# Out-projection weights split once in fp16, other orders and buffers, and the last norm's sums on TensorE

## The chip, the cores and the metric

One Trainium2 chip, one of its cores. The time is the device time of one execution in microseconds (us), the median of several runs. The engines are named as in the profile: PE is TensorE, DVE is VectorE, ACT is ScalarE, POOL is GpSimd and SP is SyncE, which here issues the DMAs, in order, in one queue.

## The reference, cut to what matters

One inference step of one layer with 2048 prompt tokens and 32 sample tokens, 1024 wide:

```python
u = rmsnorm(x, norm_mix_pre)
p = u @ w_in                                   # 3592 columns: two head groups
o_a = rmsnorm(o_a, gdn_norm_w) * silu(z)       # 4 heads of 128, gated delta rule
o_b = rmsnorm(o_b, attn_norm_w)                # 8 heads of 64, banded attention
mix = concat([o_a, o_b]) @ w_out
x = x + rmsnorm(mix, norm_mix_post)
u = rmsnorm(x, norm_ffn_pre)
gate, up = split(u @ w_gate_up)                # 2 x 2816 columns
h = gelu(causal_dwconv(gate) + ffn_conv_b) * up
x = x + rmsnorm(h @ w_down, norm_ffn_post)
```

Results are float32. The kernel multiplies in two fp16 (or fp32r) parts, high and low: a product is the sum of three matmuls, high x high, high x low and low x high.

## The kernel before, in words

Tokens lie along the free dimension, features along the 128 partitions. Mixing runs in four blocks of 512 tokens (the first has the 32 sample tokens too, so 544, done as 2 x 272). After it the FFN runs in blocks of up to 1056 tokens, as a Strassen-like scheme of seven operands a pair of feature tiles; `build_fu` makes them, each as a high part (`fuh`, ACT) and a low part (`ful`, by a subtraction).

The order of all instructions is set when the program is built, by the planner `Sched` (from line 150): streams yield operations, and the one with the earliest estimated start goes next, ties by the number given to `spawn`. `later` and a `slack` hold a PE operation back in the estimate. Every operation passes through line 191, so the profile is read by tile names, not by lines. On the chip each engine runs its own list in order and waits by semaphores; a waiting instruction holds all that are behind it on that engine. `either(wait)` (line 1624) picks DVE or POOL by the planner's estimate.

The streams that matter here:

- `dense_stream` (line 1080): products with w_in per block (kinds G and A), and the out-projection. W(b-1), the out-projection of the block before, stands eight tiles into block b. For the last block it is cut in two: P takes the heads 0, 1, 2, 4, 5 of column tiles 2 to 7 and 0, 1, and Q the late heads 3, 6, 7, in two groups of four column tiles, head by head.
- `class Weights` (line 374): w_out is loaded for each use (70 pieces `wr` of up to 128x512), scaled with the norm weight and split to two fp32r parts: `wh` by ACT, `wl` by DVE. Each out-projection matmul has an operand `oh` or `ol` (the mixed heads, F32R) and one of these.
- `ev_mix` (line 1183) evacuates a column tile of the out-projection, ACT squares it, POOL adds the squares in `acc`, and SP stores the tile in `mixd`. `residual` then sums over partitions on PE (`one,acc`), takes the power on POOL (`rcol`) and adds to x.
- `finish` (line 2339): the final norm of an FFN block. `yacc` holds the result; squares (`fx`, ACT) are added up in `facc`, PE sums over partitions (`one,facc`), POOL takes the power (`fyc`), PE spreads the factor over the partitions (`ident,fyc`), and ACT copies it to `frb` in SBUF. Then each of the 8 tiles is scaled, added to x (`end_x`) and stored. The last block runs in three parts of 512, 256 and 256 tokens. Tiles 2, 4 and 6 go by ACT and POOL, the others by DVE.

The lines of the last block's tiles before:

```python
if fb == last and k in (2, 4, 6):
    yield act(y, y, AF.Copy, scale=f_post[:, k:k + 1])
    yield G.tensor_tensor(y, y, rb[:, c0:c0 + cn], op=OP.mult)
    yield G.tensor_tensor(x[:, :cn], x[:, :cn], y, op=OP.add)
else:
    yield V.scalar_tensor_tensor(y, y, f_post[:, k:k + 1], rb[:, c0:c0 + cn], op0=OP.mult, op1=OP.mult)
    yield V.tensor_tensor(x[:, :cn], x[:, :cn], y, op=OP.add)
```

## Time and profile before

| | |
|---|---|
| median of 3 runs | 2887.34 us (2884.07 to 2887.57) |
| the profiled execution's own time | 2881.63 us |
| its span, first to last instruction | 2879.8 us |
| mean granted TensorE clock | 0.969 |
| busy: PE / DVE / ACT / POOL | 2649.2 / 2096.1 / 1474.0 / 751.7 us |

A share is an average over the span. Mixing lies before about 1451 us, the FFN behind it. In a row of the timeline the first number is the start and the second the duration, and the brackets hold the idle time of the engine ahead of the instruction with what ended it. Where PE is slow because of its clock, the windows say so in the column of the granted clock (1.0 is full speed).

### The profile page before, as it was taken

Reading aid. Unit: us, or ns where it says so; the run is one execution under the profiler, and the core shown is the slowest. Engines: PE = TensorE matmul, PEld = TensorE weight load, DVE = VectorE, ACT = ScalarE, POOL = GpSimd, SP = SyncE. Lnnn points to the kernel's source line nnn. Section 1 sums busy time; section 2 is a strip of 40 time slices with the busy share of each in tenths; the row PEclk is TensorE's granted clock in tenths of the full one; section 3 lists DMA queues with packets and bytes.
Section 4 is the critical chain, followed back from the end, with each engine's and each line's share of the span. In section 5 each row is a group of like instructions: output and inputs, shape, how many; then the busy total and the mean of one; then the engine's idle time right before and its main releaser. Section 6 shows DMA issues by size and latency. Waiting matters only on the chain.

```text
span 2879.8 us, 53610 instructions
## 1 busy us (share of the span) xinstructions
PE 2649.2 (92%) x20044; PEld 1932.2 (67%) x20044; DVE 2096.1 (73%) x4873; ACT 1474.0 (51%) x3077; POOL 751.7 (26%) x982
## 2 busy tenths in 40 slices
PE   6888899999999989999859999999998899999995
PEld 4667658666575656666637787777777768768673
DVE  6878877588867888588688867868687636456467
ACT  5666556455655656466746764736454333223132
POOL 2322232333223421242265332322213000000004
PEclk9999999999999999999979999999999999999997
DMA  5545334575546545574635543434323433223231
GB/s 173 169 97 139 102 100 119 162 160 122 139 120 163 154 104 136 147 182 107 169 116 180 168 144 124 149 107 148 118 94 124 158 98 94 81 71 100 74 122 59
DMA packets 342199, 366.66 MB, mean 127 GB/s; under 512 B 177841, under 2 KB 241585, under 8 KB 341937
## 3 DMA queue, kind: packets, MB, share of 16 engines
q1 hardware_dynamic: 340016, 356.93, 42.9%
q0 software_dynamic: 1920, 6.29, 0.7%
q8 instruction: 157, 2.57, 0.4%
q14 instruction: 106, 0.86, 0.1%
HBM read 227.64 MB, written 98.12 MB: 113 GB/s over the span
## 4 chain that ended last, share of the span: by engine, by line
PE 72%; DVE 13%; ACT 5%; DMA 4%; issue 3%; POOL 2%; SPq 1%; DVEq 0%; ACTq 0%; POOLq 0%
PE pd L191 46%; PE pg L191 16%; PE pss L191 11%; DVE ca L191 1%; ACT wijunk L191 1%; DVE fx L191 1%; DVE wip L191 1%; SPq L191 1%; DVE fy L191 1%; DVE fg L191 1%; DVE xs L191 1%; ACT fcb L191 1%; DMA w6r<-w_gate_up 1%; DMA wir<-w_gate_up 1%; DVE fcb L191 1%
## 5 line engine op out<-in xcount | busy, mean ns | idle before, releaser
L191 PEld LDWEIGHTS <-wip 128*128 128x128 f16 x8004 | 780.0, 100 | 405.3 <-issue 91.4
L191 PEld LDWEIGHTS <-w6p 128*128 128x128 f16 x5436 | 530.1, 98 | 187.3 <-issue 17.9
L191 PE MATMUL pd<-uh,wip 128*128 128x512 f16 (+1 forms) x2240 | 615.5, 348 | 26.4 <-DVE q_parts L191 6.5
L191 PE MATMUL pd<-ul,wip 128*128 128x512 f16 (+1 forms) x1120 | 389.5, 348 | 5.8 <-DVE ul L191 5.3
L191 PE MATMUL pd<-fuh,wip 128*128 128x264 f16 (+1 forms) x1176 | 220.0, 279 | 25.4 <-ACT fuh L191 10.9
L191 PE MATMUL pd<-fuh,w6p 128*128 128x256 f16 (+1 forms) x1280 | 234.1, 275 | 8.1 <-ACT fcb L191 4.4
L191 PE MATMUL pd<-ful,w6p 128*128 128x256 f16 (+1 forms) x640 | 176.0, 275 | 1.8 <-DVE ful L191 1.8
L191 PE MATMUL pd<-ful,wip 128*128 128x264 f16 (+1 forms) x588 | 163.8, 279 | 5.9 <-DVE ful L191 5.9
L191 ACT ACTIVATE pr<-pr,mn,fac 128x640 f32<-128x640 f32 (+5 forms) x136 | 115.2, 848 | 39.1 <-DVE mn L191 38.4
L191 PE MATMUL pd<-hh,w6p 128*128 128x352 f16 (+1 forms) x480 | 127.7, 338 | 0.0
L191 PE MATMUL pg<-fuh,w6p 128*128 128x264 f16 (+1 forms) x664 | 123.6, 275 | 1.7 <-ACT fcb L191 1.2
L191 PE MATMUL pss<-fuh,w6p 128*128 128x256 f16 (+1 forms) x648 | 120.4, 277 | 2.6 <-ACT fx L191 1.1
L191 DVE SCALAR_TENSOR_TENSOR ca<-cb,convw,ca 128x512 f32<-128x512 f32 (+1 forms) x144 | 116.2, 807 | 1.2
L191 PE MATMUL pd<-oh,wh 128*128 128x512 f32 (+1 forms) x311 | 115.5, 371 | 1.3 <-ACT ca L191 0.7
L191 PE MATMUL pd<-oh,wl 128*128 128x512 f32 (+1 forms) x311 | 115.1, 370 | 0.0
L191 PE MATMUL pd<-ol,wh 128*128 128x512 f32 (+1 forms) x311 | 114.6, 368 | 0.0
L191 PE MATMUL pg<-fuh,wip 128*128 128x264 f16 (+1 forms) x576 | 110.4, 280 | 2.8 <-ACT fcb L191 1.5
L191 DVE SCALAR_TENSOR_TENSOR yacc<-pd,fdinv,yacc 128x352 f32<-128x352 f32 (+2 forms) x103 | 64.8, 632 | 65.6 <-PE pd L191 65.6
L191 POOL TENSOR_TENSOR w6c<-w6c,mhalf 128x1 f32<-128x1 f32 x68 | 55.8, 821 | 216.4 <-DVE w6c L191 199.1
L191 PE MATMUL pss<-fuh,wip 128*128 128x264 f16 (+1 forms) x584 | 109.4, 276 | 1.6 <-DVE wip L191 1.0
L191 DVE CUSTOM_DVE_ANT_0 pr<-pss,bias 128x640 f32<-128x640 f32 (+5 forms) x136 | 99.2, 730 | 13.6 <-PE pss L191 11.7
L191 POOL TENSOR_TENSOR oss<-oss,mhalf 128x2 f32<-128x2 f32 (+1 forms) x68 | 53.9, 793 | 204.6 <-DVE oss L191 142.6
(651 smaller groups left out, 6885.8 us busy)
## 6 DMA issues: line engine op xcount, KB each, us to landing
wip<-wik SPq DMA_DIRECT2D x84, 512.0 KB, 3.8
w6p<-w6kP SPq DMA_DIRECT2D x82, 256.0 KB, 2.6
w6kP<-w6p SPq DMA_DIRECT2D x80, 256.0 KB, 2.1
w6kP<-wip SPq DMA_DIRECT2D x74, 256.0 KB, 2.6
xs<-xT SPq DMA_DIRECT2D x72, 256.0 KB, 3.0
wip<-w6kP SPq DMA_DIRECT2D x72, 256.0 KB, 3.0
wir<-w_in SPq DMA_DIRECT2D x28, 512.0 KB, 4.2
wik<-wip SPq DMA_DIRECT2D x28, 512.0 KB, 5.0
```

The lines of the kernel that those rows point to most:

```text
L191: o.fn()
```

## The change

What it does:

- `WeightsOut` takes the place of `Weights`. Once, in block 0 and after the fourth `z_inv`, it loads the eight column tiles of w_out (128x1024), multiplies the rows with the norm weight (and `z_inv`), finds a scale, splits to fp16 (`wop`/`wor`) and stores to DRAM (`wok`). Each use loads its tile from there. The scale is undone at the evacuation. `oh` and `ol` become fp16.
- Q goes tile by tile, with its three late heads together.
- The residual of the last block has the priority and slack of the other blocks'.
- More buffers: `u_s` three each, attention's `ph`, `pl` and `tl` two, `fx` six from the start of the FFN (before: three, and three more only when mixing's memory was freed).
- The low parts and one subtraction in `build_fu` go by `either`.
- In the last block's `finish` the factor stays in PSUM and is read there (`of[c0]`), every tile is scaled by DVE, the adds to x go by `either(0.0)`, and for parts 2 and 3 PE adds up the squares itself: for each tile and 128 tokens one product of the squares with a column of ones (`one,fx`).

```diff
-    W = Weights()
+    class WeightsOut(Weights16):
...
+            self.raw = slots(pool, "wor", 2, [128, 1024])
+            self.parts = slots(pool, "wop", 2, [128, 2, 1024], F16)
...
+        def make(self):
+            yield "need", "gnw"
+            for h in range(4):
+                yield "need", ("z_inv", h)
+            for i, h in enumerate(HEADS):
+                c = self.rows[:, i:i + 1]
+                if h < 4:
+                    yield V.scalar_tensor_tensor(c, gnw, 1.0 / G16, z_inv[:, h:h + 1], op0=OP.mult, op1=OP.mult)
+                else:
+                    yield V.tensor_scalar(c, anw, 1.0 / A16, None, op0=OP.mult)
+            spawn(self.lane(range(0, KT, 2)), 2)
+            spawn(self.lane(range(1, KT, 2)), 2)
+
+        def lane(self, cts):
+            for ct in cts:
+                r = yield from self.raw.get()
+                p = yield from self.parts.get()
+                r3 = r.rearrange("p (h m) -> p h m", m=128)
+                yield dma(out=r3, in_=I["w_out"][ct])
+                yield either(0.0).tensor_tensor(r3, r3, self.rows[:, :, None].to_broadcast([128, 8, 128]), op=OP.mult)
+                c = yield from self.cols.get()
+                d = yield from self.cols16.get()
+                yield from scale_of(r, self.junk, c, d, self.inv[:, ct:ct + 1], None)
+                self.cols16.put(d)
+                yield act(p[:, 0], r, AF.Copy, scale=c[:, 2:3])
+                yield V.scalar_tensor_tensor(p[:, 1], r, c[:, 2:3], p[:, 0], op0=OP.mult, op1=OP.subtract)
+                self.cols.put(c)
+                self.raw.put(r)
+                self.kept[ct] = dram.tile([128, 2, 1024], F16, name=f"wok{ct}")
+                yield dma(out=self.kept[ct], in_=p)
+                self.parts.put(p)
+                mark(("wo made", ct))
+            self.parts.put((yield from self.raw.get()).bitcast(F16).rearrange("p (x n) -> p x n", x=2))
...
+        def load(self):
+            for i, (ct, h0, n) in enumerate(self.pieces):
+                yield "need", ("wo made", ct)
+                p = yield from self.parts.get()
+                yield dma(out=p[:, :, :n * 128], in_=self.kept[ct][:, :, h0 * 128:(h0 + n) * 128])
+                self.ready[i] = p
+                mark(("wo", i))
...
-                of = {}
-                for ct in range(j, j + 4):
-                    of[ct] = (yield from banks.get()) if ct >= HELD else parts[ct]
+                wh, wl = yield from WO.get(p0)
+                ps = (yield from banks.get()) if j >= HELD else parts[j]
                 for i, h in enumerate(LATE_HEADS):
-                    wh, wl = yield from W.get(p0 + i)
-                    for ct in range(j, j + 4):
-                        yield from by_head(of[ct], h, wh[:, ct - j, :], wl[:, ct - j, :], n, ct >= HELD and i == 0,
-                                           h == LATE_HEADS[-1])
-                        if h == LATE_HEADS[-1]:
-                            ev = ev_mix(b, ct, acc, left, *((homes[ct], parts[ct]) if ct >= HELD else (f["cb"],)))
-                            spawn(evac(ev, of[ct], 0, n), 0)
-                    W.put(p0 + i)
+                    yield from by_head(ps, h, wh[:, i, :], wl[:, i, :], 0, n, j >= HELD and i == 0, h == LATE_HEADS[-1])
+                WO.put(p0)
+                ev = ev_mix(b, j, acc, left, *((homes[j], parts[j]) if j >= HELD else (f["cb"],)))
+                spawn(evac(ev, ps, 0, n), 0)
...
-                spawn(residual(b, acc), 2 if b == NB - 1 else 5)
+                spawn(residual(b, acc), 5)
-        sl = 0.0 if b == NB - 1 else 3000.0
+        sl = 3000.0
...
-    u_s = [slots(s2, f"u{j}_", n, [128, BT]) for j, n in enumerate((2, 2, 2, 2))]
+    u_s = [slots(s2, f"u{j}_", n, [128, BT]) for j, n in enumerate((3, 3, 3, 3))]
...
-    a_ph, a_pl, a_th, a_tl = (slots(s2, x, n, [128, 640], F16) for x, n in (("ph", 1), ("pl", 1), ("th", 2), ("tl", 1)))
+    a_ph, a_pl, a_th, a_tl = (slots(s2, x, n, [128, 640], F16) for x, n in (("ph", 2), ("pl", 2), ("th", 2), ("tl", 2)))
...
-        f["x"] = slots(b1, "fx", 3, [128, MX])
+        f["x"] = slots(b1, "fx", 6, [128, MX])
...
-        f["x"].put(*slots(b2, "fy", 3, [128, MX]).free)
...
-                def parts(i, src, low=V):
+                def parts(i, src):
-                    yield low.tensor_tensor(u[i][1], src, u[i][0], op=OP.subtract)
+                    yield either(POOL_LAG).tensor_tensor(u[i][1], src, u[i][0], op=OP.subtract)
-                yield G.tensor_tensor(x0[:, h2], x4[:, h2], x0[:, h2], op=OP.subtract)
+                yield either(POOL_LAG).tensor_tensor(x0[:, h2], x4[:, h2], x0[:, h2], op=OP.subtract)
-                yield from parts(T3, x0[:, h2], G)
-                yield from parts(B22, x4[:, h2], G)
+                yield from parts(T3, x0[:, h2])
+                yield from parts(B22, x4[:, h2])
...
-            if 0 < c0 < parts[-1][0]:
-                yield "need", ("acc", fb, parts[-1][0])
             y = yacc[k][:, c0:c0 + cn]
-            if fb == last and k in (2, 4, 6):
-                yield act(y, y, AF.Copy, scale=f_post[:, k:k + 1])
-                yield G.tensor_tensor(y, y, rb[:, c0:c0 + cn], op=OP.mult)
-                yield G.tensor_tensor(x[:, :cn], x[:, :cn], y, op=OP.add)
+            if fb == last:
+                yield V.scalar_tensor_tensor(y, y, f_post[:, k:k + 1], of[c0][:, :cn], op0=OP.mult, op1=OP.mult)
+                yield either(0.0).tensor_tensor(x[:, :cn], x[:, :cn], y, op=OP.add)
             else:
                 yield V.scalar_tensor_tensor(y, y, f_post[:, k:k + 1], rb[:, c0:c0 + cn], op0=OP.mult, op1=OP.mult)
                 yield V.tensor_tensor(x[:, :cn], x[:, :cn], y, op=OP.add)
...
+            for _ in range(nc_):
+                p = yield from banks.get()
+                ps.append(p)
+            for k in range(KT):
+                yield "need", ("y", fb, k, c0)
+                sq = yield from sqs.get()
+                yield act(sq[:, :cn], yacc[k][:, c0:c0 + cn], AF.Square)
+                for c in range(nc_):
+                    yield mm(ps[c][:, 0:1], sq[:, c * 128:c * 128 + 128], one, start=(k == 0), stop=(k == KT - 1))
+                sqs.put(sq)
+            for c in range(nc_):
+                yield V.tensor_scalar(rc[:, i + c:i + c + 1], ps[c][:, 0:1], 1.0 / DM, EPS, op0=OP.mult, op1=OP.add)
+                banks.put(ps[c])
+            yield G.tensor_tensor(yc[:, i:i + nc_], rc[:, i:i + nc_], mhalf[:, 0:nc_], op=OP.pow)
+
         def part(c0, cn):
             ac = acc[:, c0:c0 + cn]
             for k in range(KT):
-                spawn(one(k, c0, cn), 2)
+                spawn(one_tile(k, c0, cn), 2)
+            if fb == last:
+                i = c0 // 128
+                if c0 > 0:
+                    yield from sums_of_last(c0, cn)
+                else:
+                    yield from sums(c0, cn, ac)
+                    yield from rstd_cols(ac, cn, yc[:, i:], rc[:, i:], slack)
+                p = yield from banks.get()
+                for c in range(cn // 128):
+                    yield mm(p[:, c * 128:c * 128 + 128], yc[:, i + c:i + c + 1].to_broadcast([128, 128]), ident, start=True,
+                             stop=True)
+                of[c0] = p
+                mark(("rb", fb, c0))
+                yield "need", lambda: left_of[c0] == 0
+                banks.put(p)
+                return
```

PE at the end of the last block, before: behind the last real products stand the spreading of the first part's factor, and then for either smaller part its sum and its spreading (`fy` are operands, `wip` weights).

```order
L191 MATMUL pss<-fy_16217,wip_171 128x256
L191 LDWEIGHTS wip_171
L191 MATMUL pss<-fy_16217,wip_171 128x256
L191 MATMUL pd_106<-ident,fyc 128x128 x4
L191 MATMUL pd_104<-one,facc_16226 128x1 x2
L191 MATMUL pd_105<-ident,fyc 128x128 x2
L191 MATMUL pg_109<-one,facc_16226 128x1 x2
L191 MATMUL pd_107<-ident,fyc 128x128 x2
```

PE at the end, now:

```order
L194 MATMUL pd_107<-one,fx_15017 128x1
L194 MATMUL pss<-one,fx_15017 128x1
L194 MATMUL pg_108<-one,fx_15017 128x1
L194 MATMUL pd_105<-one,fx_15017 128x1
L194 MATMUL pd_107<-one,fx_15017 128x1
L194 MATMUL pd_105<-one,fx_15017 128x1
L194 MATMUL pd_107<-one,fx_15017 128x1
L194 MATMUL pd_105<-one,fx_15017 128x1
L194 MATMUL pd_104<-ident,fyc 128x128 x2
L194 MATMUL pd_107<-one,fx_15017 128x1
L194 MATMUL pd_105<-one,fx_15017 128x1
L194 MATMUL pss<-ident,fyc 128x128 x2
```

The sums of squares are products with `fx`, each for one tile's squares, of which more stand between the last real products, and the first part's spreading stands ahead of them.

PE where mixing ends, before: three of the FFN's first products, of which 18 stand behind the last Q product, then the residual's sum and spreading.

```order
L191 MATMUL pss<-fuh_0_15110,wip_172 128x264
L191 LDWEIGHTS wip_172
L191 MATMUL pss<-ful_0_15114,wip_172 128x264
L191 LDWEIGHTS wip_172
L191 MATMUL pss<-fuh_0_15110,wip_172 128x264
L191 MATMUL pd_106<-one,acc_130 128x1 x4
L191 MATMUL pd_104<-ident,rcol 128x128 x4
L191 LDWEIGHTS wip_171
L191 MATMUL pd_107<-fuh_1_15087,wip_171 128x264
```

And now:

```order
L194 MATMUL pd_107<-oh_135,wor_176 128x512
L194 LDWEIGHTS wor_176
L194 MATMUL pd_107<-ol_143,wor_176 128x512
L194 LDWEIGHTS wor_176
L194 MATMUL pd_107<-oh_135,wor_176 128x512
L194 LDWEIGHTS ones_84
L194 MATMUL pd_105<-w6d_14459,ones_84 128x1
L194 MATMUL pd_107<-one,acc_124 128x1 x4
L194 LDWEIGHTS wip_165
L194 MATMUL pss<-fuh_0_15042,wip_165 128x264
L194 LDWEIGHTS wip_165
```

The residual's sum stands right behind the last Q product (`oh`, `wor`), ahead of the first FFN product.

SP at the same place, before: the loads of x1 for the first FFN block (`fx`; six loads of `fxr` stand just ahead), two pieces of w_out, and then the stores of the Q results (`mixd`).

```order
L191 DMA fx_15060<-x1d_92 128x512
L191 DMA wr_117<-w_out 128x4x128
L191 DMA fx_15060<-x1d_93 128x512
L191 DMA fx_15060<-x1d_92 128x32
L191 DMA fx_15061<-x1d_92 128x512
L191 DMA fx_15061<-x1d_93 128x512
L191 DMA fx_15061<-x1d_92 128x32
L191 DMA w6kP_1_15217<-w6p_15072 128x1024
L191 DMA wr_118<-w_out 128x4x128
L191 DMA mixd_99<-fcb_15056 128x512
L191 DMA mixd_99<-fcb_15057 128x512
L191 DMA mixd_99<-xs_129 128x512
```

And now:

```order
L194 DMA mixd_99<-fcb_15009 128x512
L194 DMA wop_178<-wok_5274 128x2x384
L194 DMA mixd_99<-fcb_15010 128x512
L194 DMA mixd_99<-xs_122 128x512
L194 DMA wor_176<-wok_5328 128x2x384
L194 DMA mixd_99<-ca_117 128x512
L194 DMA fxr_15006<-x1d_92 128x512
L194 DMA fxr_15006<-x1d_93 128x512
L194 DMA fxr_15006<-x1d_92 128x32
L194 DMA fxr_15007<-x1d_92 128x512
```

Four stores of Q results and two loads of out-projection weights now stand ahead of the first load of `fxr`.

## Rows read from the trace of the kernel before

**Rows 1.** The page's busy line and one line of its DMA issues.

```profile
PE 2649.2 (92%) x20044; PEld 1932.2 (67%) x20044; DVE 2096.1 (73%) x4873; ACT 1474.0 (51%) x3077; POOL 751.7 (26%) x982
...
wik<-wip SPq DMA_DIRECT2D x28, 512.0 KB, 5.0
```

**Rows 2.** Windows: us, each engine's busy us (instructions), clock, DMA share, GB/s.

```profile
0.00:456.00 456.00, 386.27 (x3074) 280.91 (x3075) 352.71 (x1101) 277.75 (x662) 132.98 (x232) 0.96 0.45 129
...
400.00:1400.00 1000.00, 954.11 (x6867) 638.98 (x6866) 768.38 (x1928) 574.02 (x1248) 299.62 (x352) 0.98 0.54 137
...
1451.00:1510.00 59.00, 26.97 (x141) 18.74 (x140) 52.17 (x57) 23.27 (x42) 38.13 (x24) 0.65 0.33 105
```

**Rows 3.** Timeline, PE, the last real product: start us, duration us, instruction xcount.

```profile
2841.51 0.49 PE L191 MATMUL pss<-fy,wip 128*128 128x256 f16 x3
```

**Rows 4.** Timeline, PE, 1179 to 1218: products of either kind in a row.

```profile
1179.49 0.39 PE L191 MATMUL pd<-ol,wh 128*128 128x512 f32 x1
...
1181.79 0.39 PE L191 MATMUL pd<-oh,wl 128*128 128x512 f32 x1
...
1214.76 0.38 PE L191 MATMUL pd<-ul,wip 128*128 128x512 f16 x1
...
1217.35 0.38 PE L191 MATMUL pd<-ul,wip 128*128 128x512 f16 x1
```

**Rows 5.** Lines by form, PE, whole run: busy us, mean ns | idle before.

```profile
L191 PE MATMUL pd<-uh,wip 128*128 128x512 f16 x1344 | 433.3, 385 | 7.3 <-DVE q_parts L191 5.5 <-ACT cb L191 0.8 <-ACT uh L191 0.6
...
L191 PE MATMUL pd<-oh,wh 128*128 128x512 f32 x183 | 77.4, 423 | 1.3 <-ACT ca L191 0.7 <-ACT xs L191 0.6
```

**Rows 6.** Lines by form, DVE, whole run.

```profile
L191 DVE SCALAR_TENSOR_TENSOR wl<-wr,c_gdn_norm_w,wh 128x512 fp32r<-128x512 f32 x26 | 19.5, 750 | 11.9 <-ACT wh L191 11.8
...
L191 DVE SCALAR_TENSOR_TENSOR wip<-wir,wic,wip 128x1024 f16<-128x1024 f32 x28 | 35.8, 1280 | 4.6 <-ACT wip L191 4.4
```

**Rows 7.** Timeline, PE, 1450 to 1505, [idle before <-releaser].

```profile
1450.91 0.40 PE L191 MATMUL pd<-oh,wl 128*128 128x512 f32 x1
...
1459.26 0.59 PE L191 MATMUL pd<-one,acc 128*128 128x1 f32 x2 [5.51 <-POOL acc L191]
...
1504.28 0.38 PE L191 MATMUL pd<-fuh,wip 128*128 128x264 f16 x1 [3.28 <-ACT fcb L191]
```

**Rows 8.** Timeline, DVE, 1439 to 1495.

```profile
1439.27 1.32 DVE L191 SCALAR_TENSOR_TENSOR fxr<-fxr,ffn_scaled,frb 128x1056 f32<-128x1056 f32 x1
...
1494.81 0.49 DVE L191 SCALAR_TENSOR_TENSOR fcb<-pss,w6inv,fcb 128x264 f32<-128x264 f32 x1 [0.76 <-PE pss L191]
```

**Rows 9.** Lines by form, DVE, 1439 to 1495.

```profile
L191 DVE TENSOR_TENSOR ful<-fxr,fuh 128x528 f16<-128x528 f32 x10 | 11.6, 1160 | 1.9 <-ACT fuh L191 1.7
...
L191 DVE SCALAR_TENSOR_TENSOR fx<-fx,ffn_scaled,frb 128x1056 f32<-128x1056 f32 x4 | 8.5, 2134 | 0.3 <-DMA fx<-x1d 0.3
...
L191 DVE TENSOR_TENSOR fx<-fx,fx 128x528 f32<-128x528 f32 x2 | 1.4, 698 | 0.0
```

**Rows 10.** Timeline, PE and DVE, from 2841 to the end.

```profile
2852.37 1.01 PE L191 MATMUL pd<-one,facc 128*128 128x1 f32 x4 [8.74 <-DVE facc L191]
...
2863.45 0.94 DVE L191 SCALAR_TENSOR_TENSOR yacc<-yacc,c_norm_ffn_post,frb 128x256 f32<-128x256 f32 x1
...
2864.43 0.83 DVE L191 TENSOR_TENSOR end_x<-end_x,yacc 128x256 f32<-128x256 f32 x1
...
2873.80 0.47 DVE L191 SCALAR_TENSOR_TENSOR yacc<-yacc,c_norm_ffn_post,frb 128x256 f32<-128x256 f32 x1
...
2876.02 0.42 DVE L191 TENSOR_TENSOR end_x<-end_x,yacc 128x256 f32<-128x256 f32 x1
```

**Rows 11.** Timeline, DVE and POOL, at 2824.

```profile
2824.28 0.75 DVE L191 SCALAR_TENSOR_TENSOR yacc<-pd,fdinv,yacc 128x512 f32<-128x512 f32 x1 [0.46 <-PE pd L191]
...
2824.50 2.62 POOL L191 TENSOR_TENSOR facc<-facc,fx 128x512 f32<-128x512 f32 x2 [20.73 <-ACT fx L191]
```

**Rows 12.** Timeline, PE, at 456: the first out-projection product.

```profile
456.46 0.48 PE L191 MATMUL pd<-oh,wh 128*128 128x272 f32 x1
```

187 lines of the change are left out of this document (77 added, 110 removed).

## The prediction

> **What bounds the kernel now.** I read the page first, then the windows, then the timeline at the two places where TensorE (PE) stops. The page gives PE 2649.2 us of 2879.8, or 92%, and VectorE (DVE) 2096.1, 73% [rows 1]. An average over stages says little, so the windows come next [rows 2]. From 400 to 1400 us PE is busy 954.11 of 1000, with DVE at 768.38: PE bounds, and shorter matmuls there come back as time unless DVE's chains lie just under them. From 0 to 456, up to the first out-projection product, DVE is busy 352.71 of 456: of any 150 us there it has some 34 to spare. From 1451 to 1510, where mixing ends and the feed-forward part (FFN) begins, PE is busy only 26.97 of 59 and the clock granted to it is 0.65 on the mean, between its two levels of 1.2 and 2.4 GHz, after PE had stood idle for much of the stretch; meanwhile DVE has 52.17 of 59: DVE bounds this stretch. At the end the last product ends at 2842.0 [rows 3], with 37.8 us still to go to the end of the span. Those belong to DVE, GpSimd (POOL) and ScalarE.
>
> Durations are from the profiled execution: 2881.63 us, span 2879.8. The median shown is 2887.34, so 5.7 more; the sum is made against 2881.6 and 5.7 is added at the end.
>
> **Out-projection matmuls.** 576 of 512 columns and 384 of 272 columns go from 4-byte operands to fp16. Back to back the 4-byte ones start every 0.230 us (1179.49 to 1181.79, ten steps), fp16 ones every 0.216 (1214.76 to 1217.35, twelve steps) [rows 4]. The difference, 0.0144 x 576, is 8.3; for 272 columns, scaled by columns, 0.0077 x 384 is 2.9. That makes 11. The mean durations, 423 against 385 ns [rows 5], give 0.038 x 576 = 22, with the 2.9 some 25. Starts are what PE's time is made of, so the value lies near the lower one. I add a few us for the waits on weight pieces that end, and take **15** (11 to 25).
>
> **Splitting the weights.** 70 ScalarE and 70 DVE instructions per run go, of 0.75 us on DVE for the commonest form [rows 6], some 52 us of DVE. PE covers them today, so by themselves they are worth nothing. What comes is one making: eight tiles of 128x1024, on DVE each a split of 1.28 us as that of w_in [rows 6], a scaling of about as much (some on POOL) and small work, about 3.3 us, or 26 in all. That fits the spare time of the 150 us ahead of W(0) [rows 2] if it falls well. Each tile is stored and read again, 5.0 us for a store of its size [rows 1]. The bounds are 0, when all is covered, and 12, half of DVE's 26; I take **3 lost**, nearer to the spare time that the row shows.
>
> **From mixing to FFN.** Today PE reaches the sum of squares (one, acc) and waits 5.51 us for POOL, and DVE works from the first scaling at 1439.27 to the first FFN evacuation at 1494.81, 55.5 us [rows 7, 8]. Of this, contention is a good part: fx scalings take 2134 ns against 1320 where POOL is still, ten ful lows 1160 against 698 for an operation of that size without POOL [rows 8, 9]: 4 x 0.81 + 10 x 0.46 is 7.8 us. The change puts the lows and subtractions of this first FFN block on DVE (12 more instructions, 8.4 us by the 0.70 of [rows 9]) but takes the four weight splits off it and runs the first operands first: up to the first evacuation DVE's order adds up to about 39 us, uncontended. The loads of x1 for it now stand on SP behind the stores of the first Q results, where they stood ahead of them. So the build starts near the last Q product and not 11 us ahead of it. From Q's last product (started at 1450.91, [rows 7]) to the first evacuation that is 39 to 40 instead of 43.9 us. PE's sum now stands right behind the last Q product, with nothing to do in the wait, but the first operands wouldn't be ready either. I take **8**: 4 from this, 4 from weight pieces and attention's second buffers before it. Bounds: if contention stays, 55.5 from Q's end is 12 lost, less the 4, so 8 lost; if POOL stays clear and the loads land early, 18 gained.
>
> **Six fx buffers from the start of FFN.** The wait of 3.28 us on fcb at 1504.28 [rows 7] falls where the next FFN tiles want buffers that are still held; with a like one behind it I take **5** (0 to 8). More u and attention buffers let streams run further ahead; no row prices that: between 0 and the 46 us that PE idles in 400 to 1400 [rows 2]. DVE's chains order most of these, so I take nothing.
>
> **The end.** Removed: 14 DVE adds of squares, on which PE waits (8.74 us at 2852.37, [rows 10]), and three copies of the factor. Added: 32 one-column products, two records each, of 0.25 us after idle time (1.01 for four, [rows 10]). Some 18 of them stand ahead of the last real product, with half of that, PE being busy, some 4 us; the rest hide beside ScalarE's squares. From there on DVE has 5 scalings of 512 at 0.75 [rows 11], 16 of 256 at 0.48, 7 adds of 256 at up to 0.83 [rows 10] and small work: about 19 us. POOL has 8 adds of 512 at 1.31 [rows 11], 9 of 256, taken at 0.75, and two powers, taken at 1 each: 19 us, behind the first scaling and so 20. With 3.4 us from the last end on DVE (2876.44, [rows 10]) to the span's end as today, the end comes at 2842 + 4 + 20 + 3.4 = 2869 against 2879.8: **10** (5 to 14). Why 0.75 and 0.48: an STT that reads PSUM took 0.75 at 2824.28 while POOL was adding [rows 11]. The nearest rows the other way are scalings of 256 that read the factor in SBUF, 0.94 beside POOL and 0.47 without it [rows 10]; were the new ones slowed like those, 16 x 0.46 and 5 x 0.75 would cost some 11 more, and the gain here would be nothing.
>
> The Trainium skill, page "SBUF — State Buffer", section "Who interferes with whom", says that a DVE instruction with at most one SBUF input does not contend with GpSimd, while one with two does. The trace agrees on both sides [rows 10, 11]. By this rule the scalings are free and the 7 DVE adds beside POOL's adds are what the change has against itself: 7 x 0.41, or 2.9 us, already in the sum; by the slow row alone the sum would be 11 worse.
>
> **Sum.** 15 - 3 + 8 + 5 + 10 = 35; 2881.6 - 35 = 2846.6, and with 5.7 for the median **2852**. All terms at their worst ends give a loss of 4 (11 - 12 - 8 + 0 + 5), at their best a gain of 65: 2891 and 2822.
>
> **Rivals.**
> *DVE's chains bound up to 1400.* If PE's shorter matmuls are only waited away (DVE 768 of 1000 speaks for it, PE's 954 against it), the 15 go, and 3 of making stay: 35 - 15 = 20, so 2867 on the median's basis; with fx worth nothing too, 2872.
> *More comes back than PE's own time.* DVE loses some 52 us of splitting and ScalarE as many instructions, and streams have more buffers. If half of the 46 us of idle PE time in 400 to 1400 goes beside the 35, that is 35 + 23 = 58, so 2829. For it: DVE is busy over three quarters there [rows 2], so that work queues on it; against: PE's waits end chains, which fewer instructions elsewhere on DVE don't shorten.
> *Slower: the making holds up W(0).* PE's order is fixed; the first out-projection product (W(0), at 456.46, [rows 12]) can't be passed. Its eight tiles need all four z_inv, then two lanes of four rounds each: scaling, sum of squares, split, store, load. If a round takes its full 26/4 us of DVE and, unhidden, 10 us of store and load [rows 1], the rounds take 4 x 16.5 = 66 us; with DVE's other streams queued in between (77% busy, [rows 2]) this can double. By today's pace, 1101 DVE instructions in 456 us [rows 2], the fourth z_inv (row 761 of DVE's new order) comes near 315 us, 140 before W(0). It decides once W(0) waits over 35 us, that is from rounds of 44 us on, and is slower by over 0.2% from 41 us of wait. At 50 us a round (200 - 140 = 60 lost, of which the 3 of making are in the sum) the time is 2852 + 57 = 2909. DVE's order speaks against it: the last split stands in row 1119, some 65 of the rows ahead of it the making's own, which by the same pace is 437 us.
> *No change.* The terms at the transition and W(0) near their bad ends, about 2885.
>
> That the change does less than it says is no rival: the order shows the fp16 products, the moved sums and the PSUM operands.
>
> **Chances and range.** Within 0.2% is 5.8 us either way, about what a measurement of this kernel can tell from no change: 2881.6 to 2893.1. The forecast (2840 to 2863) 0.53, the chain-bound case (2863 to 2881) 0.21, the large gain (2815 to 2840) 0.13, no change 0.07, slower 0.06. Faster is 0.53 + 0.21 + 0.13 = 0.87. The range reaches over most of the first three, 2826 to 2877; left out are half of the large gain, the edge of the chain-bound case, and the last two.
>
> **What would show it.** Right: out-projection matmuls at starts of 0.216; PE idle from 1451 to 1510 shorter by about 8 and the scalings there near 1.31 us; from PE's last real product to the end 24 to 28 us instead of 37.8, scalings of 256 at 0.48, no wait of PE on facc after 2842. Wrong: a PE wait of over 10 us on wop near 450; the first FFN evacuation more than 50 us after the last Q product; the time to the end of the W stages unchanged although the products are shorter; DVE scalings at the end at 0.9 in spite of PSUM.

## The result, and the profile after

The changed kernel takes **2832.66 us** (median of 4 runs, 2829.59 to 2834.9), the kernel before beside it 2886.02 (4 runs, 2884.07 to 2887.57): a ratio of 0.9813 [0.98, 0.9825], or 53 us less where 35 were forecast. The profiled execution is the one of 2834.9 us, with a span of 2833.2. The forecast was 2852, the range 2826 to 2877. Ratios and intervals, here and below, leave out executions far above the others of their kernel; there are two, one of wo_q (2961.74) and one of tail_sbuf (11219.02).

| | before | after |
|---|---|---|
| W(0), first start / last end | 456.5 / 525.0 | 475.8 / 537.6 |
| last product of Q ends | 1451.3 | 1426.7 |
| first FFN evacuation | 1494.8 | 1465.4 |
| last real product ends | 2842.0 | 2809.9 |
| end of the span | 2879.8 | 2833.2 |

Differences of neighbouring lines say where the 46.6 us of span went. W(0) ends 12.6 *later*; from there to Q's end 37.2 are gained; from Q's end to the first evacuation 4.8 (43.5 to 38.7); from there to the last real product 2.7; behind it 14.5 (37.8 to 23.3).

The page's busy line of the changed kernel (against [rows 1]):

```profile
PE 2638.1 (93%) x20108; PEld 1888.8 (67%) x20108; DVE 2034.2 (72%) x4855; ACT 1449.3 (51%) x3019; POOL 749.5 (26%) x981
```

Windows of the changed kernel, columns as in [rows 2]: up to W(0), the mixing blocks, from W(0)'s end to Q's end, and from Q's last product to the first FFN evacuation. Behind them, from W(0)'s end to Q's end in the kernel before:

```profile
0.00:476.00 476.00, 400.06 (x3097) 289.94 (x3098) 380.21 (x1162) 296.13 (x693) 151.21 (x245) 0.92 0.47 145
400.00:1400.00 1000.00, 947.81 (x6904) 602.55 (x6903) 733.82 (x1943) 567.68 (x1236) 327.66 (x372) 0.97 0.56 145
537.56:1426.74 889.18, 848.41 (x6084) 530.53 (x6081) 660.37 (x1699) 508.22 (x1087) 301.18 (x341) 0.98 0.57 147
1426.70:1465.40 38.70, 19.71 (x89) 12.79 (x88) 38.23 (x60) 19.14 (x32) 7.77 (x6) 0.60 0.46 146
```
```profile
525.02:1451.31 926.29, 871.22 (x6086) 576.28 (x6085) 718.55 (x1775) 536.39 (x1145) 286.86 (x332) 0.97 0.56 145
```

Two things are worth seeing. The stretch up to W(0) has become longer, 476 us at a clock of 0.92 where it was 456 at 0.96 [rows 2]. And from 400 to 1400 PE is idle 52.2 us, where it was 45.9; but W(0) stands 19 us later in that window. Between the same points, from W(0)'s end to Q's end, PE is busy 22.8 us less (848.41 against 871.22) and idle 14.3 less (40.8 against 55.1). From Q's end on POOL is out of the way (7.77 of 38.7) and DVE is busy almost without a break.

The timeline of PE: fp16 products of the out-projection in a row, the first one of W(0), and the sum behind Q's last product.

```profile
475.75 0.28 PE L194 MATMUL pd<-oh,wop 128*128 128x272 f16 x1
...
1131.22 0.38 PE L194 MATMUL pd<-oh,wor 128*128 128x512 f16 x1
1131.43 0.38 PE L194 MATMUL pd<-ol,wor 128*128 128x512 f16 x1
1131.65 0.59 PE L194 MATMUL pd<-oh,wor 128*128 128x512 f16 x2
1132.08 0.38 PE L194 MATMUL pd<-ol,wor 128*128 128x512 f16 x1
...
1431.09 1.87 PE L194 MATMUL pd<-one,acc 128*128 128x1 f32 x8 [4.35 <-POOL acc L194]
```

From 1131.22 to 1132.08 are four steps, 0.215 us each, where the 4-byte ones took 0.230 [rows 4]. The wait of 5.51 for the sum [rows 7] is one of 4.35.

Lines by form, DVE, from 1425 to 1466, answering to [rows 9]:

```profile
L194 DVE TENSOR_TENSOR ful<-fxr,fuh 128x528 f16<-128x528 f32 x14 | 10.2, 754 | 0.0
L194 DVE TENSOR_TENSOR ful<-fx,fuh 128x528 f16<-128x528 f32 x10 | 6.8, 699 | 0.0
L194 DVE SCALAR_TENSOR_TENSOR fxr<-fxr,ffn_scaled,frb 128x1056 f32<-128x1056 f32 x4 | 5.5, 1384 | 0.3 <-DMA fxr<-x1d 0.3
L194 DVE SCALAR_TENSOR_TENSOR fx<-fx,ffn_scaled,frb 128x1056 f32<-128x1056 f32 x4 | 5.2, 1307 | 0.0
```

The scalings of `fx` take 1307 ns in place of 2134, and the lows from `fxr` 754 in place of 1160: contention with POOL is gone, as the step had it.

The end of the changed kernel, timeline of PE, DVE and POOL, answering to [rows 10, 11]:

```profile
2812.59 1.38 PE L194 MATMUL pd<-one,fx 128*128 128x1 f32 x8 [0.33 <-ACT fx L194]
...
2812.15 2.05 DVE L194 SCALAR_TENSOR_TENSOR yacc<-yacc,c_norm_ffn_post,pg 128x512 f32<-128x512 f32 x3
...
2816.44 2.83 DVE L194 SCALAR_TENSOR_TENSOR yacc<-yacc,c_norm_ffn_post,pd 128x256 f32<-128x256 f32 x7
...
2822.32 1.09 DVE L194 TENSOR_TENSOR end_x<-end_x,yacc 128x256 f32<-128x256 f32 x3
...
2823.71 3.15 DVE L194 TENSOR_TENSOR end_x<-end_x,yacc 128x256 f32<-128x256 f32 x4
...
2816.62 11.50 POOL L194 TENSOR_TENSOR end_x<-end_x,yacc 128x512 f32<-128x512 f32 x12
...
2822.34 1.65 POOL L194 TENSOR_TENSOR end_x<-end_x,yacc 128x256 f32<-128x256 f32 x1
```

The wait of 8.74 us on `facc` is gone; PE waits 0.33 for squares. Seven scalings of 256 take 2.83 us while POOL adds, 0.40 from one to the next. The last row is one of POOL's twelve adds by itself. POOL's adds run from 2816.62 to 2828.1 and DVE's end at 2826.9: POOL now ends last of the two.

### The profile page after: what moved, and what is told of

Its sections match the earlier page's. It is cut to its first block, busy times and chain, and to the rows that moved or that the text cites. A ratio compares the mean times of both kernels' runs of the same rounds, so it can differ in the third digit from the quotient of the medians.

```text
span 2833.2 us, 53532 instructions
## 1 busy us (share of the span) xinstructions
PE 2638.1 (93%) x20108; PEld 1888.8 (67%) x20108; DVE 2034.2 (72%) x4855; ACT 1449.3 (51%) x3019; POOL 749.5 (26%) x981
## 4 chain that ended last, share of the span: by engine, by line
PE 42%; DVE 6%; ACT 3%; issue 2%; DMA 1%; POOL 1%; SPq 0%; POOLq 0%; ACTq 0%; DVEq 0%
PE pd L194 21%; PE pg L194 10%; PE pss L194 10%; DVE fx L194 1%; ACT wijunk L194 1%; DVE ful L194 1%; ACT fcb L194 1%; DVE fcb L194 1%; DVE fg L194 1%; DVE hl L194 1%; POOL end_x L194 0%; DVE fxr L194 0%; DMA yT<-fxr 0%; DVE w6p L194 0%; DMA fxr<-x1d 0%
## 5 line engine op out<-in xcount | busy, mean ns | idle before, releaser
L194 PE MATMUL pd<-uh,wip 128*128 128x512 f16 (+1 forms) x2240 | 624.0, 348 | 20.7 <-DVE q_parts L194 8.3
L194 PE MATMUL pd<-fuh,w6p 128*128 128x256 f16 (+1 forms) x1200 | 216.8, 274 | 7.5 <-ACT fcb L194 3.0
L194 PE MATMUL pd<-ful,w6p 128*128 128x256 f16 (+1 forms) x600 | 164.4, 274 | 0.9 <-DVE ful L194 0.9
L194 PE MATMUL pd<-hh,w6p 128*128 128x352 f16 (+1 forms) x560 | 147.6, 338 | 0.3 <-DVE w6inv L194 0.3
L194 PE MATMUL pss<-fuh,w6p 128*128 128x264 f16 (+1 forms) x704 | 132.7, 276 | 9.5 <-ACT fcb L194 5.7
L194 ACT ACTIVATE wijunk<-fx 128x528 bf16<-128x528 f32 (+1 forms) x88 | 55.8, 634 | 123.9 <-DVE fx L194 118.4
L194 PE MATMUL pg<-fuh,wip 128*128 128x256 f16 (+1 forms) x600 | 117.2, 280 | 0.0
L194 PE MATMUL pss<-ful,w6p 128*128 128x264 f16 (+1 forms) x352 | 97.0, 276 | 0.0
L194 PE MATMUL pd<-hl,w6p 128*128 128x352 f16 (+1 forms) x280 | 94.7, 338 | 0.0
L194 PE MATMUL pg<-ful,w6p 128*128 128x264 f16 (+1 forms) x344 | 94.4, 274 | 0.0
```

The costliest lines, as they stand in the source:

```text
L194: o.fn()
```

## The experiments

The theory at the start was the prediction's sum: products and making together worth 12, the more buffers nothing, the rest 23. The rival: the buffers carry the gain. It was followed by the question why the new weights without the buffers cost time. In what follows W(0) is the first out-projection product's start in the profile.

**wo_only: the weights alone.** The kernel before with `WeightsOut`, fp16 products and the tile order of Q, and nothing else of the change (the edit in part):

```diff
-    W = Weights()
+    class WeightsOut(Weights16):
...
+            spawn(self.lane(range(0, KT, 2)), 2)
+            spawn(self.lane(range(1, KT, 2)), 2)
```

> The kernel before with the fp16 weights alone (made once, Q tile by tile); buffers, FFN and the end as before. Theory P (the shorter products pay by themselves: PE was 16 us less busy up to Q's end in the changed kernel): 2861 to 2870 us, Q ends 16 to 25 us earlier than 1451, and the end stays at 37 to 39 us behind the last real product. Rival B (the mixing gain comes from the added u and attention buffers): 2875 us or more, Q's end within 10 us of 1451.

Measured: 2912.99 us (2901.06 to 2920.75), 1.0085 [1.0063, 1.0108]: 27 us **slower** than before. Theory P is out; the rival's time holds, its end of Q doesn't, which comes 24 us late (1475.2). Once W(0) is done, the new weights do pay: from its end to Q's end it takes 910.1 us against 926.3, 16 less. But W(0) starts at 506.9, 50 late, and ends 40 late. In the windows, before and then wo_only, up to W(0), a piece early on, and the piece from 456 to 510:

```profile
100.00:240.00 140.00, 120.58 (x1054) 95.67 (x1054) 114.68 (x369) 93.84 (x228) 38.68 (x69) 0.96 0.42 110
...
456.00:510.00 54.00, 53.44 (x509) 50.89 (x506) 37.19 (x89) 35.12 (x82) 13.34 (x13) 1.00 0.47 122
```

```profile
0.00:507.00 507.00, 416.46 (x3154) 300.08 (x3155) 384.69 (x1173) 304.08 (x702) 158.67 (x252) 0.91 0.47 137
...
100.00:240.00 140.00, 121.36 (x949) 95.77 (x949) 104.00 (x339) 85.66 (x207) 39.26 (x66) 0.84 0.35 102
...
456.00:510.00 54.00, 38.98 (x256) 24.16 (x255) 38.41 (x130) 29.68 (x71) 17.40 (x21) 0.71 0.47 124
```

From 100 to 240 PE is as busy as before (121.36 and 120.58), but with 949 products in place of 1054, at a granted clock of 0.84 in place of 0.96. Up to W(0) it is idle 90.5 us where it was 69.7 [rows 2], 21 more, and busy 416.46 where it was 386.27, 30 more. In these 30 the granted clock is 0.91 in place of 0.96 and 80 more matmuls run; the runs don't divide them. The program gives W(0) to PE's list only when all eight heads of block 0 and the heads of its sample tokens are there (`dense_stream`), and in wo_only it is a head and not its weights that comes last: ScalarE writes the last attention head of block 0 right ahead of it. ScalarE, then PE, of wo_only:

```profile
505.98 0.28 ACT L194 ACTIVATE oh<-pd 128x128 f16<-128x128 f32 x1 [0.26 <-PE pd L194]
```
```profile
506.86 0.28 PE L194 MATMUL pd<-oh,wop 128*128 128x272 f16 x1
```

W(0)'s first weights were back from DRAM at 474.7, and the last piece of the making was split at 473.9 and stored at 483.3. In all fourteen profiles W(0) starts within 6 us of that head's end. So block 0's chain of attention items sets W(0), in all but ph3 (below), and the making acts through it.

**bufs_old, u_old, pp_old: the buffers.** The changed kernel with the old counts of `u`, of attention's `ph`, `pl`, `tl`, or of both (bufs_old). The changed kernel also has attention items wait for both halves of an earlier item, where the kernel before waited for the second alone; these three runs keep that.

```diff
-    u_s = [slots(s2, f"u{j}_", n, [128, BT]) for j, n in enumerate((3, 3, 3, 3))]
+    u_s = [slots(s2, f"u{j}_", n, [128, BT]) for j, n in enumerate((2, 2, 2, 2))]
...
-    a_ph, a_pl, a_th, a_tl = (slots(s2, x, n, [128, 640], F16) for x, n in (("ph", 2), ("pl", 2), ("th", 2), ("tl", 2)))
+    a_ph, a_pl, a_th, a_tl = (slots(s2, x, n, [128, 640], F16) for x, n in (("ph", 1), ("pl", 1), ("th", 2), ("tl", 1)))
```

> The changed kernel with two u buffers each and one ph, pl and tl. Theory P (buffers matter little beside the products): 2833 to 2841 us, Q's end within 8 us of 1427. Rival B (they gave the mixing gain): 2846 us or more, Q's end at 1440 or later.

> The changed kernel with two u buffers each again; ph, pl and tl stay at two. Theory U (the third u buffer lets block 0's products run ahead; with it the fourth z_inv came at 319 us, without it at 344 to 351): W(0) ends near 554 and not 530 to 538, in all 2855 to 2880 us. Rival A (attention's second buffers made the 55 us): within 8 us of 2833.

> The changed kernel with one ph, pl and tl again; three u buffers stay. Theory U: W(0) ends where it does in the changed kernel (530 to 538); the 13 us of the last mixing block (246 against 259 from W(2)'s end to Q's end) are attention's, so 2840 to 2852 us. Rival A (attention's buffers made most of it): 2860 us or more. Rival 0 (all is the u buffers'): within 4 us of 2833.

Measured: bufs_old 2888.43, 1.0001 [0.9991, 1.001]; u_old 2860.57, 0.9908 [0.989, 0.9926]; pp_old 2868.76, 0.9934 [0.9911, 0.9957]. Against 2832.66 the old counts cost 56, 28 and 36. Either kind alone gives only a part. The rival of bufs_old and theory U of u_old hold; of pp_old rival A holds: theory U had W(0)'s end unmoved (530 to 538), and it came at 569.8. From W(0)'s end to Q's end bufs_old takes 907.8 us, with PE idle 57.2; the changed kernel takes 889.2, idle 40.8. So nearly all that the buffers give in that stretch is idle time of PE. The windows from 100 to 240 of u_old, pp_old and the changed kernel show what the third `u` does:

```profile
100.00:240.00 140.00, 125.59 (x956) 99.32 (x956) 104.03 (x353) 86.18 (x212) 40.63 (x64) 0.79 0.38 105
```
```profile
100.00:240.00 140.00, 126.21 (x1114) 102.73 (x1114) 115.56 (x365) 95.43 (x223) 38.49 (x67) 0.94 0.45 135
```
```profile
100.00:240.00 140.00, 130.61 (x1174) 106.22 (x1174) 118.52 (x377) 99.90 (x233) 43.70 (x77) 0.95 0.47 141
```

In the five profiles with the new weights and two `u` slots PE does 949 to 1010 products there, at a clock of 0.79 to 0.93; in seven of the eight with three slots 1114 to 1206, at 0.94 to 0.99 (the eighth is make_early, below, which brings the making into this stretch: 1010). The fourth `z_inv`, on which the making waits, comes at 318.9 in the changed kernel and at 358.4 in u_old. The second slot of `ph` and `pl` works later: pp_old is not far back at 240, but starts W(0) at 512.3.

**make_light and wo_light: the work of the making taken out,** once with the buffers (the changed kernel), once without (wo_only). Only loads, two ScalarE copies and the store remain, so that neither computes the layer (the edit in part):

```diff
-                yield either(0.0).tensor_tensor(r3, r3, self.rows[:, :, None].to_broadcast([128, 8, 128]), op=OP.mult)
...
-                yield from scale_of(r, self.junk, c, d, self.inv[:, ct:ct + 1], None)
...
-                yield act(p[:, 0], r, AF.Copy, scale=c[:, 2:3])
-                yield V.scalar_tensor_tensor(p[:, 1], r, c[:, 2:3], p[:, 0], op0=OP.mult, op1=OP.subtract)
+                yield act(p[:, 0], r, AF.Copy, scale=1024.0)
+                yield act(p[:, 1], r, AF.Copy, scale=0.5)
```

> The changed kernel, whose making leaves out the scaling of w_out's rows, the search for a scale and the split (no work on VectorE or GpSimd): ScalarE writes two fp16 copies, the stores and loads stay. Theory W (the work of the making, some 26 us on VectorE between 357 and 465, holds up the chains of block 0 and 1): W(0) ends at 515 to 526, in all 2812 to 2824 us. Rival L (stores, loads and the order of W(0) cost it, not the work): W(0) ends at 530 to 540 and the time is within 5 us of 2833.

> The kernel before with fp16 products of w_out and nothing else of the change, as in wo_only (2912.99 us, first out-projection product at 506.9), but with the making of the fp16 pieces cut to its loads, two ScalarE copies and the store: the scaling by the norm's rows, the search for the columns' scale and the split are left out, so what it computes is not the product with w_out. Theory L (the work of the making on DVE and POOL holds up the attention items of block 0, whose last head is written 0.6 us before that product): the product starts at 470 to 480 and the time is 2875 to 2890. Theory S (the making's loads and stores, and what else stands in SP's one queue, hold up attention's transposes): the work is not the cause, the product stays within 10 us of 506.9 and the time is 2903 to 2915.

Measured: make_light 2827.67, 0.9788 [0.9771, 0.9805], 5 less than the changed kernel, with overlapping intervals, and W(0) ends at 527.8, which lies between the two theories. wo_light 2898.44, 1.0037 [1.0022, 1.0052], W(0) at 492.5: 14.5 less than wo_only, and W(0) 14.4 earlier. That lies between the two theories. Without the buffers the work costs some 14, with them perhaps 5; but some 36 us of W(0)'s delay stay without any of it. Most of that is older than the making: the head that ends at about 372 in wo_only and 371 in wo_light, the thirteenth of twenty, ended at 338.0 before, and the making's first load goes out only at 379.2 in wo_only. ScalarE in before, wo_only and wo_light, and SP in wo_only:

```profile
337.79 0.17 ACT L191 ACTIVATE oh<-pd 128x32 fp32r<-128x32 f32 x1
```
```profile
371.91 0.18 ACT L194 ACTIVATE oh<-pd 128x32 f16<-128x32 f32 x1
```
```profile
370.85 0.18 ACT L194 ACTIVATE oh<-pd 128x32 f16<-128x32 f32 x1
```
```profile
379.22 0.90 SPq L194 DMA_DIRECT2D wor<-w_out  x2
```

**wo_q: the making's transfers off SP.** wo_only, with the eight loads and eight stores on POOL's queue:

```diff
-                yield dma(out=r3, in_=I["w_out"][ct])
+                yield G.dma_start(out=r3, in_=I["w_out"][ct])
...
-                yield dma(out=self.kept[ct], in_=p)
+                yield G.dma_start(out=self.kept[ct], in_=p)
```

> As wo_only, but the making's eight loads and eight stores are issued by POOL in place of SP, so that they stand in no transposes' way; its work stays. Theory S: the sum of the waits of attention's transposes between their operand and their issue, up to 510 us, falls from 95 us to under 70 (48 in the kernel before), the first out-projection product starts at 470 to 488 and the time is 2877 to 2895. Theory L: whatever the transposes' waits do, that product stays within 10 us of 506.9 and the time is 2903 to 2918.

Measured: 2907.75, 1.006 [1.0043, 1.0076]; W(0) at 497.3; the waits of the high halves' transposes (`th<-ph`) add up to 82.9 us, from 95.2. The interval overlaps that of wo_only (1.0063 to 1.0108). Theory S misses all three of its numbers; theory L, that these transfers aren't what holds W(0) up, meets both of its own, W(0) narrowly (9.6 us earlier, which may be the clock's doing: see the last section). The one queue does hold transposes up, but the longest time behind something else. SP in wo_only, around the probabilities that ScalarE had written at 350.6:

```profile
354.70 9.38 SPq L194 DMA_DIRECT2D xs<-xT  x5
366.22 0.38 SPq L194 DMA_DIRECT2D xs<-cache_v  x1
369.36 0.33 SPq L194 DMA_DIRECT2D xs<-xT  x1
369.74 1.18 SPq L194 DMA_TRANSPOSE th<-ph  x1
```

The transpose goes out 19.2 us after its operand was there, behind loads of x and of the cache, which stand on SP in the kernel before too. In the changed kernel the waits are even longer in sum (124.1 us, 120.5 with what overlaps counted once), and W(0) comes earlier all the same.

**make_early: the making earlier.** The changed kernel, with `z_inv` applied in the recurrence, so that the making can start behind the second `z_inv` in place of the fourth (the edit in part):

```diff
-            for h in range(4):
-                yield "need", ("z_inv", h)
+            yield "need", ("z_inv", 1)
```

> The changed kernel with z_inv applied in the gated delta step as in the kernel before, so that the making needn't wait for the fourth z_inv: it starts after the second and stands some 400 instructions earlier on VectorE. Theory W-place (the making costs because it falls between 357 and 465, where block 0 meets block 1): 2812 to 2824 us, W(0) ends at 515 to 526. Theory W-any (VectorE is loaded everywhere in the first 450 us, so its 26 us cost wherever they lie): within 6 us of 2833, with the idle time of PE moved to 150 to 270.

Measured: 2846.38, 0.986 [0.9842, 0.9878], 14 **slower** than the changed kernel, which neither theory had, although W(0) starts at 468.1 and ends 5 us earlier. At Q's end the lead is gone (1428.8 against 1426.7), and nearly all of the loss arises in the FFN: from the first evacuation to the last real product 1358.4 us against 1344.4, a stretch that the edit doesn't touch.

It is not alone in this. Differences of the profiles in us, the last run against the kernel before, the others against the changed kernel:

| | W(0) ends | Q ends | the FFN stretch | end of the span |
|---|---|---|---|---|
| bufs_old | +16.5 | +35.0 | +11.2 | +43.0 |
| u_old | +12.8 | +22.0 | +14.1 | +31.8 |
| pp_old | +32.3 | +36.6 | +14.8 | +44.9 |
| make_early | -4.9 | +2.1 | +14.0 | +14.7 |
| make_light | -9.8 | -11.5 | +3.7 | -7.6 |
| wo_only | +40.0 | +23.9 | +15.5 | +35.2 |

So in all but make_light 11 to 16 us of what the edit of mixing costs lie in the FFN. The operations there are the same, but the planner orders them anew: of the first 1680 DVE instructions of the stretch, taken by their tiles' names, bufs_old, u_old, pp_old and make_early have 111 to 189 at the same place as the changed kernel, and make_light, ph3 and tail_old, which lose under 4 us there, over 1500. In wo_only PE is idle 52.8 us in the stretch where it was 46.1, at a clock of 0.982 where it was 0.989. What in the new orders costs this is left open.

**ph3: a third slot for `ph` and `pl`,** in the changed kernel:

```diff
-    a_ph, a_pl, a_th, a_tl = (slots(s2, x, n, [128, 640], F16) for x, n in (("ph", 2), ("pl", 2), ("th", 2), ("tl", 2)))
+    a_ph, a_pl, a_th, a_tl = (slots(s2, x, n, [128, 640], F16) for x, n in (("ph", 3), ("pl", 3), ("th", 2), ("tl", 2)))
```

> The changed kernel with a third slot for each half of attention's probabilities ahead of the transposes (ph, pl), the transposed ones (th, tl) at two as they are. The second slot was worth some 36 us (pp_old). If attention's chain in block 0 still waits for a slot (the making ends at 464 us there, the last head at 472.5), the first out-projection product comes at 455 to 468 in place of 475.8 and the time is 2813 to 2826. If two slots were enough, or the two transposed slots are now the tighter ones, the product stays within 6 us of 475.8 and the time is 2827 to 2838.

Measured: **2822.58**, 0.9775 [0.9757, 0.9793], the fastest complete kernel of the study, 10 less than the changed one. W(0) starts at 465.4, and Q ends at 1418.0. Both numbers were told in advance by the theory of attention's chain, but W(0) and Q's end lie close to those of tail_old (469.6 and 1417.0), which has two slots, so the profiles alone don't show the way. What they show is that the chain is no longer the last: attention's last head ends at 459.51, and W(0) follows the delta rule's heads of the sample tokens, which end at 465.37. ScalarE, then PE, of ph3:

```profile
465.03 0.34 ACT L194 ACTIVATE oh<-g_tmp 128x32 f16<-128x32 f32 x2
```
```profile
465.36 0.43 PE L194 MATMUL pd<-oh,wop 128*128 128x272 f16 x1
```

So in this profile still more slots could bring W(0) forward only if they sped up that chain too, which was not tried.

**tail_old, fx_old, tail_sbuf: the other steps.** In the changed kernel, tail_old has the old `finish`; fx_old three `fx` buffers at the start of the FFN and three more later, as before; tail_sbuf keeps PE's sums, but copies the factor to SBUF (the first and last edit in part):

```diff
-                if c0 > 0:
-                    yield from sums_of_last(c0, cn)
...
+            if fb == last and k in (2, 4, 6):
+                yield act(y, y, AF.Copy, scale=f_post[:, k:k + 1])
+                yield G.tensor_tensor(y, y, rb[:, c0:c0 + cn], op=OP.mult)
```
```diff
-        f["x"] = slots(b1, "fx", 6, [128, MX])
+        f["x"] = slots(b1, "fx", 3, [128, MX])
...
+        f["x"].put(*slots(b2, "fy", 3, [128, MX]).free)
```
```diff
-                of[c0] = p
-                mark(("rb", fb, c0))
-                yield "need", lambda: left_of[c0] == 0
+                yield act(rb[:, c0:c0 + cn], p[:, :cn], AF.Copy)
...
+                of[c0] = rb[:, c0:c0 + cn]
```

> The changed kernel with the end of the kernel before (squares added by DVE, factor copied to SBUF, tiles 2, 4 and 6 by ScalarE and GpSimd). Theory P (the end is worth what the traces show, 37.8 less 23.3 us): 2845 to 2849 us, the last real product where it is in the changed kernel, some 37 us before the end of the span. Rival (part of that came from work done ahead of the last product): under 2840.

> The changed kernel with three fx buffers from the start of the FFN and three more when mixing's memory is free. Theory P: 2 to 5 us slower, 2835 to 2838, lost between the first FFN evacuation and the first product with hh (117.6 us in the changed kernel, 122.6 before). Rival (nothing waits on these buffers): within 2 us of the changed kernel, and the 117.6 stays.

> The changed kernel, but at the end ScalarE copies each part of the factor from PSUM to SBUF, and the last scalings read it there. The port rule of the prediction (a DVE instruction with two SBUF inputs is slowed while POOL adds): scalings of 256 beside POOL's adds take 0.8 to 0.95 us in place of 0.48, those of 512 1.2 to 1.5 in place of 0.75, and with 16 and 5 of them the end comes 6 to 11 us later: 2839 to 2844. Rival (POOL's adds, back to back from 2808.7 to 2828.1 in the changed kernel, set the end, and DVE has room): the scalings are slower but the end moves by under 4 us: 2830 to 2837.

Measured: tail_old 2843.16, 0.985 [0.9835, 0.9866], 10.5 more, between the theory and the rival; in the profiles 37.6 us from the last real product to the end against 23.3. fx_old 2835.23, 0.9842 [0.9819, 0.9865], 2.6 more by the medians, as its theory had it, and 8 by the ratios, two of its five runs being 10 to 17 us above the others; the intervals overlap, so they don't tell it from nothing. tail_sbuf 2838.51, 0.9831 [0.9815, 0.9846], 5.9 more, between its two theories, which overlaps as well, with 26.8 us of tail. PE in tail_old has the old waits again:

```profile
2807.14 1.01 PE L194 MATMUL pg<-one,facc 128*128 128x1 f32 x4 [7.05 <-DVE facc L194]
...
2816.37 1.01 PE L194 MATMUL pd<-one,facc 128*128 128x1 f32 x4 [5.84 <-DVE facc L194]
```

tail_sbuf did not become the test it was meant as. With the factor in SBUF the planner gave every add of the end to DVE and none to POOL, so nothing contended. Two rows of DVE in it:

```profile
2836.72 0.87 DVE L194 SCALAR_TENSOR_TENSOR yacc<-yacc,c_norm_ffn_post,frb 128x256 f32<-128x256 f32 x2
2837.51 0.75 DVE L194 TENSOR_TENSOR end_x<-end_x,yacc 128x256 f32<-128x256 f32 x2
```

So it shows what POOL's share of the adds and the direct reading of the factor are worth together: an end on DVE alone, with ScalarE's three copies of the factor, is 3.5 us longer by the profiles. For the price of SBUF operands beside POOL there are rows of tail_old, DVE with POOL adding and then without:

```profile
2829.21 0.94 DVE L194 SCALAR_TENSOR_TENSOR yacc<-yacc,c_norm_ffn_post,frb 128x256 f32<-128x256 f32 x1
...
2830.94 0.47 DVE L194 SCALAR_TENSOR_TENSOR yacc<-yacc,c_norm_ffn_post,frb 128x256 f32<-128x256 f32 x1
```

## Why the prediction was right, and where it was wrong

The sign and the range hold; the way to them holds in part. By medians, in the order in which the runs undo the change:

| step | forecast | measured |
|---|---|---|
| products and making (wo_only less before) | -12 | +26.7 |
| residual, `fx`, low parts, end (bufs_old less wo_only) | -23 | -24.6 |
| `u` and attention buffers (after less bufs_old) | 0 | -55.8 |
| sum | -35 | -54 |

The parts don't simply add (the two kinds of buffers cost 28 and 36 singly, 56 together), so the table holds in this order alone. The second row also holds the longer waits of attention items, which the prediction had no term for. That it comes out near the forecast is in part luck: the profiles put 13 of the difference of these two kernels ahead of Q's end and 7 in the FFN stretch, where its terms had 4 and 5. Two terms were mis-sized, in opposite directions, and the sum came out nearer than its terms; that, too, is luck.

- **The products, 15: right in size.** Start to start, by the median of each kind, the 512 columns went from 0.233 to 0.216 and the 272 from 0.126 to 0.116: 576 x 0.017 + 384 x 0.010 = 14. In wo_only 16 us come back from W(0)'s end to Q's end; that stretch holds only the 576, for 10 of the 16, and the rest isn't told apart.
- **The making, 3 lost: wrong.** Its 26 us of DVE were set against DVE's spare time ahead of W(0) [rows 2]. In the profiles of wo_only and the kernel before, 35.2 us apart, W(0) ends 40.0 later, 16 come back up to Q's end, 15.5 are lost in the FFN stretch, and 4 come back around it. Of the 50 us of W(0)'s later start 14 are the work (wo_light). Some 34 arise before the making's first load. There PE does less work at a lower clock, in an order that the planner changed; what in that order costs it is not settled: wo_q speaks against the making's own transfers on SP. Up to 10 of the 50 may be that one profile's low clock (last section). So the step that failed is to price the making by DVE's spare time alone: the work is the smaller part, and the larger one is what the new order does ahead of W(0) and in the FFN.
- **Buffers, 0: wrong.** The prediction said that no row prices them, and put them between 0 and 46. It then took 0 because DVE's chains order the streams, and gave no room to the bound in the sum. The runs price them at 56. In the profiles 16.5 of the 43.0 are there at W(0)'s end, 18.5 more come up to Q's end, nearly all of it idle time of PE, and 11 in the FFN stretch. A row to look at was that of W(0): it follows the last head of block 0 by 3 us in the kernel before too, so whatever lets attention run ahead moves W(0).
- **Mixing to FFN, 8: half seen.** The 4 from Q's end to the first evacuation came as 4.8, of which 2.5 are there in wo_only (41.0), without the step's lows and residual. The other 4, for the weight pieces and buffers ahead of it, can't be told from the terms above.
- **`fx` buffers, 5: not contradicted, not shown.** 2.6 by the medians, 8 by the ratios. In the profiles, first evacuation to first product of `hh`, fx_old has 124.4 us against 117.7. The wait of 3.28 that the term was read from ends with ScalarE's evacuation to `fcb` [rows 7]; the row names no `fx` buffer.
- **The end, 10: right,** 10.5 by the medians, 14.5 by the two profiles. PE no longer waits for `facc`, and the scalings took 0.40 to 0.48 beside POOL. By the rule of the Trainium skill, page "SBUF — State Buffer", section "Who interferes with whom", that the prediction drew on, a DVE instruction with at most one SBUF input does not contend with GpSimd, and one with two contends with a GpSimd instruction that reads SBUF. The trace agrees for the scalings (a duration of 0.94 in tail_old, 0.48 here). For the adds it agrees as well, with either engine paying: four of DVE's took 3.15 us beside POOL's, and three others 1.09, but meanwhile POOL's add at 2822.34 took 1.65, where those just ahead of it took 0.74.

Of the rivals, **more comes back than PE's own time** (2829) is nearest to the time, and part of its mechanism is there: it had 23 us of PE's idle time coming back, and from W(0)'s end to Q's end 14.3 did. It is the buffers that bring them, not the missing splits: the idle time of that stretch is 55.1 us before, 56.6 in wo_only and 57.2 in bufs_old. **The making holds up W(0)** is real. In the changed kernel it is 19 us of later start, outweighed by 37 from W(0)'s end to Q's. In wo_only, without the buffers, it decides together with the FFN's loss, and the kernel is slower. But it comes by way of attention's chain, not by the weights: the fourth `z_inv` came at 318.9 (forecast 315) and the last split ended at 465.7 (437), still ahead of the last head. **DVE's chains bound** fell: the shorter products came back as time.

What stays open: the low parts, the residual's priority and the order of Q were not tried one by one, nor were the buffers alone in the kernel before, and nothing holds the planner's order of the FFN fixed. Single profiles of one and the same program differ by some 13 us: tail_old and tail_sbuf are the changed kernel up to its last tokens, and their Q ends at 1417.0 and 1429.8, where the changed kernel's ends at 1426.7. So differences below 10 us at W(0), and 13 at Q's end, are not relied on here; make_early's start of W(0) and ph3's end of Q are among them.

## What to carry to other kernels

Before new work is put ahead of a fixed point on the busiest engine, find what arrives last at that point now, and ask what the new work does to that chain; free time on the engine that does the work says little. Where a chain passes through single buffers and one queue in order, a second or third slot is the cheapest answer, and a term "no row prices it" should widen the sum and not enter as zero. Undo each part of a change by itself: a gain of 53 was here a loss of 27 and two gains of 25 and 56. And where a planner orders the whole program, compare the stretches that an edit does not touch as well: here they held 11 to 16 us of the price of five of them.

## What was not expected of the hardware

A busy share doesn't show a low clock. From 100 to 240 us PE was busy 121 of 140 in wo_only and in the kernel before, but did 949 products in the one and 1054 in the other, at a granted clock of 0.84 and 0.96. Ahead of it stands a wait of PE that the kernel before doesn't have, in the timeline of wo_only:

```profile
102.60 0.39 PE L194 MATMUL pd<-uh,wip 128*128 128x272 f16 x1 [5.14 <-DVE q_parts L194]
```

From 100 to 120 the clock was 0.57 there and 0.91 before. But the changed kernel has the same wait (4.94 us) and a clock of 0.67 behind it, and makes the time up by 240 with its third `u` slot. So the wait and the clock behind it do not explain wo_only alone. Nor does the one always bring the other: all profiles but that of the kernel before have this wait, of 4.4 to 5.6 us, and in tail_old, bufs_old, wo_q and make_early the clock behind it is 0.91. That gives a price. With one program up to the FFN, the changed kernel (0.67), fx_old (0.74) and tail_sbuf (0.57) start W(0) at 475.8, 474.2 and 475.6, and tail_old (0.91) at 469.6, some 6 us earlier. Likewise wo_only (0.57) starts it at 506.9, and its near twins wo_q and bufs_old (0.91) at 497.3 and 496.3. Why the clock falls in one execution and not in another is left open.
